# Queries of blocks 0 to 3 projected ahead of the third group's keys in a hybrid attention / mLSTM diffusion step

## The chip, the cores and the metric

The kernel runs on one core of one Trainium2 chip. The metric is device time in microseconds (us) of one execution; lower is better. The kernel before takes 1570.68 us, the median of three runs (1569.95 to 1571.53).

## The reference: what is computed

One layer of a hybrid backbone over 128 context tokens and 1024 latent tokens with 1024 features each. Cut to what matters here:

```
sh1, sc1, g1, sh2, sc2, g2 = split(silu(cond) @ w_ada + b_ada)       # adaLN, per kind of token
h  = rmsnorm(x, norm1_w) * (1 + sc1) + sh1
aq, ak, av, mq, mk, mv, mo, mg = split(h @ w_in)                      # widths 512,128,128,4 x 512,16
aq = rmsnorm(aq per head) ; ak = rmsnorm(ak per head)                 # 8 query, 2 key heads of 64
latent tokens: axial rotary on aq, ak; keys = own + cached
attn_o = softmax(aq ak^T / 8) av
hm  = bidirectional chunkwise mLSTM(mq, mk, mv, gates from mg)        # 4 heads of 128
x   = x + g1 * (concat(attn_o, rmsnorm(hm) * sigmoid(mo)) @ w_out)
x   = x + g2 * swiglu(rmsnorm(x) * (1 + sc2) + sh2)
```

The outputs are both token groups after a final norm, the context's keys and values, and the context's final mLSTM states.

## The kernel before

The 1152 tokens are nine blocks of 128 rows: block 0 is the context, blocks 1 to 8 are latent. Three blocks make a group (CB = 3, NCH = 3). Products of full precision are made from pairs: a float32 matrix is scaled by a power of two and split into a high float16 part and a low remainder, and each product is three matmuls (high times high, low weight times high, high weight times low).

A weight set of the input projection is an object of class `Scaled`. `ready()` loads its four raw pieces, takes sums of absolute values on ACT (L198), and finds the power of two through a small chain over DVE and PE (`power_scale`, tiles `isc` and `pv`, L164 to L176). `pairs()` makes high parts on ACT (L218, L221, L222) and low parts on DVE (L219, L137), each piece in a tile of the tag `ipair`, which has four slots. The raw pieces of all sets but the first are in the tag `iraw`, also four slots.

The stage that the change touches is the first 165 us:

- Loads on SP's queue: x of blocks 0 to 5, the key/value/gate weights (`kvg`, 272 columns), sixteen tiles of `w_ada`, x of blocks 6 to 8 (L279), then the query weights, and so on.
- Groups 0 and 1 are normalised and turned (transposed on PE, L116, copies at L371 and L372). The adaLN strips of shift and scale run on PE (L341), with a copy at L388.
- For each group c: `features(c)` forms the modulated, transposed tokens `hT` in pairs on ACT (L507) and DVE (L508, L137); then `linear_tok` projects the keys, values and gates of its three blocks (L483 to L485, 128x272). Behind the keys of group 0 stands `normalise(2)` (ACT squares L355, DVE scalings L358), behind those of group 1 `turn(2)`. Beside the keys of groups 1 and 2 run the steps of the query weights and of `ada`, a generator of the remaining adaLN loads (L423, 512 KB each, three buffers) and strips (L341).
- Then the pool of this stage is closed, a pool for the mLSTM is opened in its place, and the queries of all nine blocks are projected (L483 to L485, 128x512), in five groups `PAIRS` = (0, 1), (2, 3), (4,), (5, 6), (7, 8). Evacuating a group (`evac_q`) scales it (ACT, L724), normalises and rotates it over ACT, DVE and POOL (`norm_rope`, L664 to L686) and writes it to DRAM (`q_d`, L729, SP's queue).
- Beside the queries four generators are advanced, in the ratios 0.7, 1.15, 0.6, 0.3 of a step per unit of main work: `gates` (the gate chain from G to QT, L557 to L654), `ada`, `kwork` (key norms, key stacks `kst`, value parts), and the steps of the first mLSTM head's weights.
- Behind this the per-head projections (L808 to L810), the mLSTM scans and the attention follow, with PSUM pools that take the place of this stage's.

Python order gives each instruction a priority. A planner fixes each engine's order before the run from estimated times: of the instructions that it holds to be ready, the one of highest priority goes next; `hot(n)` moves the instructions inside it n places ahead. `weave(main, side, n_main, n_side)` interleaves two generators by count.

Of the kernel before, what the change touches and what calls it, by code (L numbers as in the profile page):

```python
# [19 lines left out]
P = 128  # L20
D = 1024
KD = D // P
NB = 9
# [22 lines left out]
def hybrid_step(ctx: ExitStack, tc: tile.TileContext, I: dict, O: dict):  # L46
# [11 lines left out]
    def nm(s):  # L58
        uid[0] += 1
        return f"{s}_{uid[0]}"  # L60
# [118 lines left out]
    class Scaled:  # L179
# [31 lines left out]
        def pairs(self, dve_every=2):  # L211
            out = []
            n, b = self.n, self.shape[1]
            for j, raw in enumerate(self.raws):
                w = wp.tile([P, 2, 1024], F16, name=nm("ipair"), tag="ipair", bufs=4)
# [162 lines left out]
    kvg_pairs = kvg.pairs(1)  # L378
# [119 lines left out]
    def features(c):  # L498
# [3 lines left out]
        for k in range(KD):  # L502
            full = p0.tile([P, CB, P], F32, name=nm("full"), tag="full", bufs=4)
            for i, n in ((0, 1), (1, 2)) if c == 0 else ((0, CB),):
                cnd = 0 if n == 1 else 1
                s, t = scale1[:, k, cnd : cnd + 1], shift1[:, k, cnd : cnd + 1]
                act(hh[:, k, i : i + n], v[:, k, i : i + n], AF.Identity, scale=s, bias=t)  # L507
                dve.tensor_scalar(out=full[:, i : i + n], in0=v[:, k, i : i + n], scalar1=s, scalar2=t, op0=ALU.mult, op1=ALU.add)  # L508
            sub(hl[:, k], full, hh[:, k], "dve")

    for c in range(NCH):
        with hot(100):
            features(c)
        prods = linear_tok(kvg_pairs, 0, 272, evac_kvg, (tuple(range(c * CB, c * CB + CB)),), bank if c == 1 else bankA)
        if c > 0:
            weave(prods, chain(steps, ada), KD, 10)
        else:
            emit(prods)
        if c == 0:
            normalise(2)  # L520
        if c == 1:
            turn(2)
    emit(steps)
    es0.close()
    mlp = es1.enter_context(tc.tile_pool(name="mlp", bufs=1, reuse_waits="tile"))
    mwh = mlp.tile([P, 512], F32, name="mwh")
    for tag, shape, bufs, dt in (("cs", [P, P + 1], CSB, F32), ("c0f", [P, P + 1], 2, F32), ("c0b", [P, P + 1], 1, F32), ("hm", [P, NB, P], 2, F32), ("ssh", [P, NB], 2, F32), ("nu", [P, 2, P + 1], 4, F32),
                                 ("it", [P, 2, P + 1], 3, F32), ("dn", [P, 2], 3, F32), ("jkh", [P, P], 1, BF16), ("sd", [P, 2, P], 4, F32),
                                 ("dt", [P, 2, P], 4, F32), ("so", [P, P], 9, F32), ("va", [P, P + 1], 9, F32), ("kT", [P, P], 9, F32),
# [1030 lines left out]
```

## Time and profile before

| | |
|---|---|
| median of three runs | 1570.68 us |
| profiled execution, own time | 1568.19 us |
| its span, first to last instruction | 1566.4 us |
| mean granted TensorE clock | 0.982 |
| PE busy | 1484.4 us (95%) |
| DVE busy | 1017.7 us (65%) |
| ACT busy | 771.7 us (49%) |
| POOL busy | 267.8 us (17%) |
| DMA moved | 236.91 MB, mean 151 GB/s |

Engines are PE (TensorE matmul), PEld (its weight loads, which overlap PE), DVE (VectorE), ACT (ScalarE), POOL (GpSimd) and SP (SyncE, which issues most DMAs); SPq is SP's queue. L483 is line 483 of the kernel before. In a row `out<-in` names the tiles, `x8` the count, and what stands in brackets is how long the engine stood idle before and what ended that. Ends of matmuls are modelled, so a busy PE is not PE at its peak; distances between starts tell the rate.

### The profile page before, as it was taken

The numbers are of one execution on the slowest core, as the hardware profiler recorded it, in microseconds if no ns is written. First come the engines' busy times: TensorE is split into PE (matmuls) and PEld (weight loads), VectorE is DVE, ScalarE is ACT, GpSimd is POOL, SyncE is SP. The second block draws the span as 40 slices with busy tenths as digits, with TensorE's granted clock in tenths as the row PEclk, the third lists the DMA queues.
The fourth block names the chain that finished last, engine by engine and source line by source line (L and its number), as shares of the span: only waits on it lengthen the run. The fifth ranks groups of instructions, "written<-read, shape, count | busy, mean of one in ns | idle before, by whom it ended". The sixth has DMA issues, their size and how long they took to land.

```text
span 1566.4 us, 23369 instructions
## 1 busy us (share of the span) xinstructions
PE 1484.4 (95%) x8539; PEld 1244.8 (79%) x8539; DVE 1017.7 (65%) x2007; ACT 771.7 (49%) x1413; POOL 267.8 (17%) x354
## 2 busy tenths in 40 slices
PE   6899999999999689999999999999999999999997
PEld 3544567677766468898998989989898989999996
DVE  4878554837669576677555677878866585554554
ACT  4754465847656344545432444556552443323333
POOL 0213333322343242100110101000010101001110
PEclk9899999999999799999999999999999999999999
DMA  9564323523657748767554547878773545534441
GB/s 362 177 190 156 100 68 41 130 38 68 122 148 170 254 80 201 182 182 170 153 154 144 152 126 237 195 172 178 176 169 114 168 129 175 162 117 139 148 139 63
DMA packets 387881, 236.91 MB, mean 151 GB/s; under 512 B 170198, under 2 KB 346790, under 8 KB 387766
## 3 DMA queue, kind: packets, MB, share of 16 engines
q1 hardware_dynamic: 385110, 231.84, 54.2%
q10 hardware_dynamic: 2656, 3.58, 1.1%
q8 instruction: 67, 1.10, 0.3%
q14 instruction: 48, 0.39, 0.1%
HBM read 183.79 MB, written 13.26 MB: 126 GB/s over the span
## 4 chain that ended last, share of the span: by engine, by line
PE 80%; DVE 9%; ACT 4%; DMA 4%; issue 2%; POOL 1%; SPq 0%; ACTq 0%; DVEq 0%; POOLq 0%
PE mm L1316 12%; PE mm L1317 11%; PE mm L1315 11%; PE mm L1115 5%; PE mm L1116 5%; PE mm L1117 5%; PE S L1035 4%; PE wi L485 3%; PE wi L484 3%; PE wi L483 3%; PE mm L1147 2%; PE mm L1148 1%; PE mm L1149 1%; PE mm L116 1%; PE po L1060 1%
## 5 line engine op out<-in xcount | busy, mean ns | idle before, releaser
L152 ACT CAST whi<-raw 128x1024 fp32r<-128x1024 f32 (+1 forms) x216 | 221.9, 1027 | 415.1 <-PE mm L1316 148.8
L137 DVE TENSOR_TENSOR wlo<-raw,whi 128x1024 fp32r<-128x1024 f32 (+1 forms) x216 | 259.9, 1203 | 204.9 <-ACT whi L152 204.4
L1316 PE MATMUL mm<-aTl,whi 128*128 128x384 f32 x1056 | 355.7, 337 | 2.7 <-DVE aTl L137 2.7
L1317 PE MATMUL mm<-aTh,wlo 128*128 128x384 f32 x1056 | 354.3, 336 | 0.0
L1315 PE MATMUL mm<-aTh,whi 128*128 128x384 f32 x1056 | 353.3, 336 | 0.0
L137 POOL TENSOR_TENSOR hl<-tn,hl 128x384 fp32r<-128x384 f32 x66 | 84.1, 1275 | 840.0 <-ACT hl L1338 757.3
L1316 PEld LDWEIGHTS mm<-aTl,whi 128*128 128x128 f32 x1056 | 198.5, 188 | 3.9 <-DVE aTl L137 3.3
L1315 PEld LDWEIGHTS mm<-aTh,whi 128*128 128x128 f32 x1056 | 198.1, 188 | 0.6
L1317 PEld LDWEIGHTS mm<-aTh,wlo 128*128 128x128 f32 x1056 | 198.4, 188 | 0.0
L1116 PE MATMUL mm<-wlo,hl 128*128 128x512 f32 x372 | 145.7, 392 | 0.0
L1115 PE MATMUL mm<-whi,hl 128*128 128x512 f32 x372 | 144.3, 392 | 0.0
L1117 PE MATMUL mm<-whi,hl 128*128 128x512 f32 x372 | 143.4, 392 | 0.0
L483 PE MATMUL wi<-ipair,hT 128*128 128x384 f16 (+2 forms) x408 | 135.2, 334 | 2.0 <-ACT hT L507 1.2
L484 PE MATMUL wi<-ipair,hT 128*128 128x384 f16 (+2 forms) x408 | 135.2, 334 | 0.0
L485 PE MATMUL wi<-ipair,hT 128*128 128x384 f16 (+2 forms) x408 | 132.0, 335 | 1.0 <-DVE hT L137 1.0
L1042 DVE SCALAR_TENSOR_TENSOR pl<-pr,st,ph 128x1152 f16<-128x1152 f32 (+1 forms) x72 | 94.8, 1317 | 33.9 <-ACT ph L1041 32.5
L1041 ACT ACTIVATE ph<-pr,st 128x1152 f16<-128x1152 f32 (+1 forms) x72 | 83.8, 1164 | 27.2 <-issue 7.2
L1037 DVE TENSOR_REDUCE st<-S 128x1 f32<-128x1152 f32 (+1 forms) x72 | 88.8, 1233 | 12.5 <-PE S L1035 12.3
L1038 ACT ACTIVATE pr<-S,st 128x1152 f32<-128x1152 f32 (+1 forms) x72 | 81.3, 1129 | 31.7 <-DVE st L1037 28.0
L1035 PE MATMUL S<-kst,qT 128*128 128x384 f32 (+1 forms) x400 | 86.8, 347 | 5.0 <-ACT pr L1038 5.0
L1104 DVE TENSOR_TENSOR t<-mm,gl 128x512 f32<-128x512 f32 x102 | 68.9, 685 | 26.2 <-DMA gl<-g_d 12.5
L1117 PEld LDWEIGHTS mm<-whi,hl 128*128 128x128 f32 x372 | 69.9, 188 | 14.2
(381 smaller groups left out, 2525.0 us busy)
## 6 DMA issues: line engine op xcount, KB each, us to landing
raw<-in_w_gu_dram SPq DMA_DIRECT2D x132, 512.0 KB
raw<-in_w_down_dram SPq DMA_DIRECT2D x60, 512.0 KB
a<-in_w_ada_dram SPq DMA_DIRECT2D x24, 512.0 KB
gl<-g_d SPq DMA_DIRECT2D x36, 256.0 KB
aw<-in_w_ada_dram SPq DMA_DIRECT2D x16, 512.0 KB
iraw<-in_w_in_dram SPq DMA_DIRECT2D x32, 256.0 KB
raw<-in_w_out_dram SPq DMA_DIRECT2D x12, 512.0 KB
x<-in_x_sample_dram SPq DMA_DIRECT2D x11, 512.0 KB
```

Source lines behind the costliest of these rows:

```text
L137: (dve if eng == "dve" else pool).tensor_tensor(out=out, in0=full, in1=hi, op=ALU.subtract)
L152: nc.scalar.copy(hi[:, :n], raw[:, :n])
L483: mm(ps[:, :n], ah, wh[:, k % 2, c0 : c0 + n], start=(k == 0), stop=False)
L484: mm(ps[:, :n], ah, wl[:, k % 2, c0 : c0 + n], start=False, stop=False)
L485: mm(ps[:, :n], al, wh[:, k % 2, c0 : c0 + n], start=False, stop=(k == KD - 1))
L1035: mm(S[:, n, 0:w], qT[:, h, :], kst[kv][:, t, c0 + n * w : c0 + (n + 1) * w], start=(t == 0), stop=(t == 1))
L1115: mm(ps, ah, wh[:, k % 2, :], start=(k == 0), stop=False)
L1116: mm(ps, ah, wl[:, k % 2, :], start=False, stop=False)
L1117: mm(ps, al, wh[:, k % 2, :], start=False, stop=(k == nk - 1))
L1315: mm(ps, wh[:, k, :], th[:, k, :], start=(k == 0), stop=False)
L1316: mm(ps, wh[:, k, :], tl[:, k, :], start=False, stop=False)
L1317: mm(ps, wl[:, k, :], th[:, k, :], start=False, stop=(k == KD - 1))
```

## The change

Four parts, all in the first stage:

1. The object of the query weights is made, and its loads are issued, ahead of the loads of x for blocks 6 to 8. Its sums and its scale are emitted ahead of the features.
2. The pairs of the key weights get tiles of their own (`kpair0` to `kpair3`) in the stage's pool `p0`, instead of the four `ipair` slots.
3. The order around the keys is written out. `normalise(2)` follows the keys of group 0, its ACT instructions behind the last one of `features(0)`; then the query weights' pairs are made and the first head's weights are loaded; the keys of group 1 are woven with four steps of `ada`, which has had one step before; `turn(2)`, `features(2)`; then the queries of blocks 0 to 3 and, behind these, the keys of group 2, woven with 27 steps of `ada`.
4. The remaining five blocks' queries (24 units instead of 40) run beside the four generators, with ratios 1.17, 1.15, 1.0 and 0.5.

`features` also returns its last ACT instruction. The loop over groups goes away; the opening of the mLSTM pool and the load of `mwh` stand behind the keys of group 2 as before. The diff's core:

```diff
-        def pairs(self, dve_every=2):
+        def pairs(self, dve_every=2, home=None):
...
-                w = wp.tile([P, 2, 1024], F16, name=nm("ipair"), tag="ipair", bufs=4)
+                w = home(j) if home else wp.tile([P, 2, 1024], F16, name=nm("ipair"), tag="ipair", bufs=4)
...
+    q_group = Scaled([[(full_view, rows_of(j)[:, :, 0:512])] for j in range(4)], (2, 512))
+    q_steps = q_group.ready()
+    next(q_steps)
     for b in range(2 * CB, NB):
         load_x(b)
...
-    kvg_pairs = kvg.pairs(1)
+    kvg_pairs = kvg.pairs(1, lambda j: p0.tile([P, 2, 544], F16, name=f"kpair{j}"))
...
-    groups_in = [Scaled([[(full_view, rows_of(j)[:, :, 0:512])] for j in range(4)], (2, 512))] + [head_group(h) for h in range(NH)]
-    steps = groups_in[0].ready()
-    next(steps)
+    groups_in = [q_group] + [head_group(h) for h in range(NH)]
+    emit(q_steps)
...
-    for c in range(NCH):
-        with hot(100):
-            features(c)
-        prods = linear_tok(kvg_pairs, 0, 272, evac_kvg, (tuple(range(c * CB, c * CB + CB)),), bank if c == 1 else bankA)
-        if c > 0:
-            weave(prods, chain(steps, ada), KD, 10)
-        else:
-            emit(prods)
-        if c == 0:
-            normalise(2)
-        if c == 1:
-            turn(2)
-    emit(steps)
...
+    next(ada)
     qp = es_r.enter_context(tc.tile_pool(name="qp", bufs=1, side="right", reuse_waits="tile"))
...
+    def keys(c):
+        return linear_tok(kvg_pairs, 0, 272, evac_kvg, (tuple(range(c * CB, c * CB + CB)),), bank if c == 1 else bankA)
+
+    with hot(100):
+        last = features(0)
+    emit(keys(0))
+    with tc.issue_after(last):
+        normalise(2)
+    with hot(100):
+        features(1)
+    w_q = q_group.pairs()
+    q_group.inverses()
+    steps = groups_in[1].ready()
+    next(steps)
+    weave(keys(1), ada, KD, 4)
+    turn(2)
+    with hot(100):
+        features(2)
+    evac = evac_q(qp, qcc, qss, qw)
+    weave(chain(linear_tok(w_q, 0, 512, evac, PAIRS[:2]), keys(2)), ada, 3 * KD, 27)
...
-    w_q = groups_in[0].pairs()
-    groups_in[0].inverses()
-    steps = groups_in[1].ready()
-    next(steps)
-    weave(linear_tok(w_q, 0, 512, evac_q(qp, qcc, qss, qw)), beside((gates, 0.7), (ada, 1.15), (kwork, 0.6), (steps, 0.3)), 40, 40)
+    weave(linear_tok(w_q, 0, 512, evac, PAIRS[2:]), beside((gates, 1.17), (ada, 1.15), (kwork, 1.0), (steps, 0.5)), 24, 24)
```

More of the change, by code (lines that the diff above doesn't have):

```diff
@@ L506, in features @@
                 s, t = scale1[:, k, cnd : cnd + 1], shift1[:, k, cnd : cnd + 1]
[L507 removed]
+                last = act(hh[:, k, i : i + n], v[:, k, i : i + n], AF.Identity, scale=s, bias=t)
                 dve.tensor_scalar(out=full[:, i : i + n], in0=v[:, k, i : i + n], scalar1=s, scalar2=t, op0=ALU.mult, op1=ALU.add)
             sub(hl[:, k], full, hh[:, k], "dve")
[L511 to L531 removed]
+        return last.ins
     def gate_work(mlp):
@@ L731, in evac_q @@
         return evac
-    dma(mwh, I["mlstm_norm_w"][0:1, :].to_broadcast([P, 512]))
-    dve.tensor_scalar(out=mwh, in0=mwh, scalar1=0.5, scalar2=None, op0=ALU.mult)
     def qcol(i, d, b, h):
```

12 lines of the change are left out of this document (10 added, 2 removed).

## The prediction

> **What bounds the kernel now.** I read the page's head first, then busy time by stretches of the span, cut where the order of the work changes: features and keys of the first two groups (46 to 67.7 us), turn, features and keys of the third (67.7 to 93, "the front"), the query projection (93 to 165.2, "the tail"), then everything behind it.
>
> ```profile
> span 1566.4 us, 23369 instructions
> PE 1484.4 (95%) x8539; PEld 1244.8 (79%) x8539; DVE 1017.7 (65%) x2007; ACT 771.7 (49%) x1413; POOL 267.8 (17%) x354
> ...
> 46.00:67.70 21.70, 20.42 (x144) 14.86 (x144) 21.70 (x58) 18.16 (x45) 6.61 (x6) 0.83 0.44 117
> 67.70:93.00 25.30, 20.67 (x174) 12.93 (x174) 22.38 (x75) 16.01 (x27) 4.83 (x5) 0.93 0.63 197
> 93.00:165.20 72.20, 66.28 (x407) 30.68 (x406) 55.20 (x189) 38.02 (x76) 16.63 (x11) 0.98 0.54 162
> 165.20:480.00 314.80, 305.80 (x1998) 219.21 (x1998) 187.19 (x499) 198.06 (x559) 108.88 (x222) 0.99 0.39 89
> ```
>
> The columns are the stretch, its length, busy time (and instructions) of PE, PEld, DVE, ACT and POOL, the granted clock, DMA share and GB/s. PE carries the kernel at 95%. From 46 to 67.7 us DVE is busy for all 21.70 us and sets the pace. From 67.7 on PE sets it, but with holes: 25.30 - 20.67 = 4.6 us in the front and 72.20 - 66.28 = 5.9 us in the tail. From 165.2 to 480 PE is busy 97% of the time, so I take a start there that is earlier by so many us as an end earlier by as many. The waits and the clock name the holes:
>
> ```profile
> PE mm L175 <- DVE pv L164: 2.3, 2, 1.4
> PE mm L341 <- DMA a<-in_w_ada_dram: 2.2, 3, 1.1
> PE mm L116 <- DVE isc L200: 1.0, 1, 1.0
> PE wi L483 <- ACT vall L493: 0.7, 1, 0.7
> ...
> PE mm L116 <- DVE ry L133: 3.7, 1, 3.7
> PE wi L808 <- DVE QT L654: 1.6, 1, 1.6
> ...
> 68.00:70.80 2.80, 0.66 (x3) 0.47 (x3) 2.70 (x21) 1.71 (x6) 0.00 (x0) 0.95 0.00 0
> 70.80:72.70 1.90, 1.90 (x17) 0.62 (x17) 1.76 (x14) 1.56 (x2) 0.22 (x1) 0.50 0.00 0
> 72.70:75.00 2.30, 2.30 (x22) 1.54 (x19) 0.69 (x3) 1.22 (x2) 0.65 (x2) 0.73 0.77 238
> 136.00:138.60 2.60, 2.59 (x9) 1.44 (x10) 2.37 (x10) 2.54 (x4) 1.83 (x1) 0.50 1.04 347
> ```
>
> A wait row gives the total, the times, and the longest. After a hole the granted clock is 0.50 to 0.73: the front loses 1.90 x 0.50 + 2.30 x 0.27 = 1.6 us by that, the tail 2.60 x 0.50 = 1.3. So the front wastes 4.6 + 1.6 = 6.2 us and the tail 5.9 + 1.3 = 7.2; these 13.4 us are all there is to win behind 67.7 us.
>
> **The change, part by part.**
>
> *Loads.* The four query weight loads go ahead of the last three rows of x.
>
> ```profile
> 27.67 3.23 SPq L279 DMA_DIRECT2D x<-in_x_sample_dram  x3
> 34.29 4.21 SPq L193 DMA_DIRECT2D iraw<-in_w_in_dram  x4
> ...
> 40.00:46.00 6.00, 2.80 (x19) 2.44 (x19) 3.16 (x24) 4.53 (x11) 0.00 (x0) 0.77 1.05 393
> ...
> 39.60 0.58 ACT L388 COPY part<-wi 128x512 f32<-128x512 f32 x1 [9.86 <-PE wi L341]
> 45.50 11.91 ACT L507 ACTIVATE hT<-x,shift,scale 128x128 f16<-128x128 f32 x24 [0.37 <-DVE shift L402]
> ```
>
> SP issues the rows at 27.67 and the weights at 34.29, and the DMA engines are full (1.05) up to 46 us at 393 GB/s. The weights are 2.1 MB, 5.3 us at that rate; the rows come that much later, the weights 3 x 0.52 MB, 4 us, earlier. The rows' squares no longer run at 40 us but behind the first group's features, as the change orders them itself, so their lateness costs nothing. This is the one wait that is added: on ACT the squares stand behind the features that run from 45.50 to 57.4, and behind the squares stand the key evacuations and the pairs; DVE's row scalings wait for them, but DVE is full with features up to 66.6 anyway. The eight absolute-value sums move to where the squares were, with 9.86 us of ACT idle ahead of 39.60. If such a sum stands before the copy there or the first features at 45.50 in ACT's order and its weights are late, the start slips: from 0 to 1.3 us, the time of one such load at 393 GB/s. I take 0.3, as the loads come 4 us earlier. Behind it, the query weights' scale is known by about 50 us, and the waits on isc and pv at 67.7 to 70.4 (1.0 + 1.4) lose their cause.
>
> *Key weights' pairs in own tiles.* No instruction is added; the query weights' pairs no longer wait for slots which the third group's keys still read. They move from about 90 us to just behind DVE's full stretch, whose end is
>
> ```profile
> 66.57 2.07 DVE L358 TENSOR_SCALAR x<-x,ry 128x1024 f32<-128x1024 f32 x3
> ```
>
> The first piece's low part can only come behind the features and these three row scalings, near 69.5 us; PE has only adaLN strips until then. Bounds of that hole: 0.5 us (strips fill it) to 4.6 (as wide as the front's holes now). I take 2.0.
>
> *Queries of blocks 0 to 3 into the front.* The adaLN strips by forms, in the tail and in the front; the query products in the front, one of their three lines; and the starts of two of them:
>
> ```profile
> L341 PE MATMUL mm<-a,silp 128*32 128x256 f32 x128 | 10.4, 390 | 0.0
> ...
> L341 PE MATMUL mm<-a,silp 128*32 128x256 f32 x64 | 6.4, 455 | 2.2 <-DMA a<-in_w_ada_dram 2.2
> L485 PE MATMUL wi<-ipair,hT 128*128 128x512 f16 x2 | 0.8, 379 | 0.0
> ...
> 109.78 0.38 PE L483 MATMUL wi<-ipair,hT 128*128 128x512 f16 x1
> 110.00 0.38 PE L484 MATMUL wi<-ipair,hT 128*128 128x512 f16 x1
> ```
>
> Starts are 0.216 us apart, so four blocks of 24 matmuls are 4 x 24 x 0.216 = 20.7 us; some 8 of these (2 to 3 on each line, 1.7 us) ran in the front already: 19.0 us move. The third group's keys end after 1 + 4 + 27 = 32 adaLN steps of 55, some 14 of 24 loads' strips; now 64 of 192 strip matmuls, 8 loads, lie ahead of 93 us. Six loads' strips, at 10.4 / 16 = 0.65 us each, move too, and some columns, 0.5: 4.4 us. PE's work at full clock becomes 20.7 - 1.6 + 19.0 + 4.4 = 42.5 us in the front and 66.3 - 1.3 - 23.4 = 41.6 in the tail. Instructions, PSUM evacuations and DMAs stay the same in number. POOL's part of the two groups moves along, into a front where POOL is busy 4.83 of 25.30 us, at no cost.
>
> DVE decides whether PE can keep that pace:
>
> ```profile
> L679 DVE TENSOR_TENSOR nr<-qraw,ss 128x256 f32<-128x256 f32 x8 | 4.0, 553 | 2.0 <-POOL qraw L668 2.0
> L666 DVE TENSOR_REDUCE nrs<-nr 128x16 f32<-128x1024 f32 x3 | 3.6, 1217 | 1.8 <-ACT nr L664 1.8
> L131 DVE TENSOR_TENSOR rt<-ry 128x16 f32<-128x16 f32 x9 | 2.7, 304 | 0.1
> L686 DVE TENSOR_TENSOR qraw<-qraw,nr 128x1024 f32<-128x1024 f32 x1 | 1.2, 1206 | 0.0
> ```
>
> Normalising two groups of query blocks is 2 x 1.22, 24 small ones at 0.17 to 0.30 (say 0.27, 6.5), six L679 at 0.55 (3.3) and 1.9 of L686 (1.2 and half of it): 14.1 us. With one weight pair's low part (1.2, a 128x1024 operation like L686's) and adaLN's small ones some 16 us move, so the front has 22.4 + 16 = 38.4 us of DVE to 42.5 of PE (90%), the tail 39.2 to 41.6 (94%); the tail now has 55.2 to 65.0 (85%) and wastes 7.2 / 65.0 = 11%. Front: the 2.0 us hole, 0.5 where the keys' third bank waits for a query evacuation (0.7 now for its like), and a clock loss. Tail: 11% x 94/85 x 41.6 = 5.1; bounds 0.5 (no hole but the last) to 15.5 (below).
>
> *The clock.* The row at 70.8 shows 0.50 although PE, in the 2.8 us before, was busy 0.66 us and waited no more than 1.4 us at a time. So a 2 us hole can still bring slow time, and I leave half of the front's 1.6 us, 0.8. The Trainium skill, "TensorE: Matmul & The Clock Gate", section "What's actually happening", has the clock halved only after an idle window of about 3.4 us; this row does not bear that out, as the wait was shorter and broken. By that page the 0.8 would fall away and the sum come 0.8 lower; the row decides.
>
> *SP's queue.* The order of loads on it changes: four query weights earlier, the first head's eight loads at about 70 instead of 89 us, four query blocks' writes among the adaLN loads.
>
> ```profile
> SPq L423 <- PE mm L341: 41.3, 15, 12.5
> SPq L729 <- DVE qraw L686: 21.2, 4, 12.3
> ```
>
> A write waits up to 12.3 us for its normalising, and adaLN loads queue behind it. Their rate is that of the tail now (27 steps to 24 units against 1.15 to one), where PE waited for none. I take 0, bounds 0 to 5 us. The gates' and the keys' steps are only packed into 24 units instead of 40.
>
> **Sum.** Front 6.2 - (2.0 + 0.5 + 0.8) = 2.9 us won, tail 7.2 - 5.1 = 2.1 won, start 0.3 lost: 4.7 us. The profiled execution took 1568.19 us (span 1566.4), 2.5 below the median of 1570.68; the difference is put on the median: 1566.0.
>
> **Rivals.**
>
> *The gates' chain sets the end (slower).* It starts with the last keys' gate columns and ends with QT, whose copy releases PE at the stage's end (the 1.6 us wait above). The steps of PE, and the results that they use:
>
> ```profile
> 96.65 0.36 DVE L496 SCALAR_TENSOR_TENSOR G<-wi,isc,gbias 128x8 f32<-128x8 f32 x2 [0.15 <-ACT vall L493]
> 113.22 0.15 DVE L581 COPY ends<-cm 64x1 f32<-64x1 f32 x1
> ...
> 122.01 0.38 PE L116 MATMUL mm<-ident,ends 128*1 128x128 f32 x2
> ...
> 135.31 0.31 ACT L620 ACTIVATE dec<-dec 1x128 f32<-1x128 f32 x1 [7.17 <-DVE dec L619]
> ...
> 148.67 0.48 PE L624 MATMUL mm<-dec,one 1*128 1x128 f32 x2
> ...
> 151.00 0.31 ACT L639 ACTIVATE qe__1707<-qe__1707 128x128 f32<-128x128 f32 x1
> ...
> 162.53 0.31 PE L116 MATMUL mm<-ident,ai 128*128 128x128 f32 x1
> ```
>
> From 97.0 to 165.2 it takes 68 us, under 65 us of PE work. Three pauses ahead of PE's steps are 113.4 to 122.0, 135.6 to 148.7 and 151.3 to 162.5: 33 us; bare it is 35 us. Afterwards only 41.6 us of PE work cover it, while DVE's 39.2 us stand in the same queue. Should two thirds of the pauses stay, it takes 35 + 22 = 57, the tail wastes 15.5, and the kernel is 15.5 - 7.2 - 2.9 + 0.3 = 5.7 us slower: 1576. It turns to a loss when the chain is over 41.6 + 7.2 + 2.6 = 51 us. For it: DVE at 94%. Against: the pauses are PE's order, and the rates of the gates' steps are raised.
>
> *No change.* SP blocks behind a query write and PE waits some 5 us for adaLN weights in the front: 1571. For: three such waits (2.2 us) now; against: none in the tail, at the same rate.
>
> *All holes close.* DVE's moved work fits everywhere: 13.4 less 2: 1559. Against: DVE at 90% and more throughout.
>
> **How the numbers follow.** 0.2% (3.1 us) is about what a measurement tells from no change. My forecast, 1566 (1561 to 1567.5), has 0.40, all holes closed 0.15, no change 0.17, the gates' chain 0.28. Faster is then 0.55, same 0.17, slower 0.28. The range from 1558.5 to 1577 takes in the first rival's price and the full closing, and leaves out a longer chain and a gain past 12 us, 2 in 10.
>
> **What would show it.** Right: PE without waits on isc and pv near 68 us; 128x512 query matmuls from about 70 us; the third keys' end near 113; first head matmuls near 160.5 us instead of 165.2. The tail step fails if PE waits for QT or key transposes for over 10 us together; the load step if the features start after 45.8; the SP step if adaLN waits exceed 2.2 us. A shift behind 165 us of another size than at 165 would make the prediction wrong as well.

## The result, and the profile after

The changed kernel is slower: 1579.03 us (median of six runs, 1577.01 to 1580.36) against 1570.32 us for the kernel before beside it (1569.48 to 1574.25). The ratio is 1.0057, 95% interval 1.0044 to 1.0069. The forecast was 1566.0 with a range up to 1577. The profiled execution took 1578.23 us, its span is 10.0 us longer than before's. First the page's head:

```profile
span 1576.4 us, 23369 instructions
...
PE 1486.6 (94%) x8539; PEld 1245.2 (79%) x8539; DVE 1013.8 (64%) x2007; ACT 771.5 (49%) x1413; POOL 269.5 (17%) x354
```

The instructions are the same in number and the engines as busy as before; the 10 us are waiting and slow clock. To place them, I cut both spans alike into three stretches: the start (46 to 68 us), the front (68 to 132) and the tail (132 to 180). The columns are those of the prediction's table. Before:

```profile
46.00:68.00 22.00, 20.44 (x144) 14.86 (x144) 22.00 (x59) 18.46 (x46) 6.61 (x6) 0.83 0.43 116
68.00:132.00 64.00, 58.98 (x413) 29.45 (x413) 48.92 (x183) 33.29 (x63) 12.08 (x11) 0.97 0.60 184
132.00:180.00 48.00, 42.31 (x261) 22.86 (x254) 39.81 (x107) 26.43 (x49) 13.65 (x8) 0.96 0.46 139
```

After:

```profile
46.00:68.00 22.00, 15.70 (x91) 10.94 (x92) 21.64 (x70) 19.83 (x41) 8.44 (x6) 0.73 0.43 112
68.00:132.00 64.00, 64.00 (x462) 32.66 (x461) 37.83 (x114) 30.48 (x62) 10.82 (x9) 0.98 0.63 192
132.00:180.00 48.00, 37.44 (x213) 19.94 (x210) 42.76 (x153) 25.76 (x49) 12.36 (x9) 0.86 0.40 116
```

What TensorE wastes in a stretch is its length less PE's busy time multiplied by the granted clock: before 22.00 - 20.44 x 0.83 = 5.0, 6.8 and 7.4 us; after 10.5, 1.3 and 15.8. So the front wins 5.5 us, as it was meant to, the start loses 5.5 and the tail 8.4: together 8.4 of the 10.0 us are lost by 180 us. Behind that TensorE's order of instructions, from head 0's first score product on, is the old one but for three places.

The forecast had its own stages: the front up to the end of the third keys, and the tail from there to the first head product. In the changed kernel these are the stretches up to 119.4 and up to 172.4 us; the third column of busy time is DVE's:

```profile
67.70:119.40 51.70, 51.70 (x370) 27.16 (x368) 28.80 (x69) 23.94 (x49) 8.96 (x6) 0.98 0.58 178
119.40:172.40 53.00, 42.44 (x268) 21.37 (x268) 46.30 (x178) 30.66 (x61) 12.08 (x10) 0.90 0.53 159
```

The start's loss is one wait. First PE's longest between 47 and 70 us, then, in the order of time, DVE's steps of the scale's chain:

```profile
PE mm L175 <- DVE pv L164: 5.4, 1, 5.4
```

```profile
54.66 0.15 DVE L200 TENSOR_REDUCE isc<-isc 128x1 f32<-128x8 f32 x1
...
59.02 0.27 DVE L171 TENSOR_REDUCE pv<-mm 1x1 f32<-1x128 f32 x1
...
61.21 0.14 DVE L161 TENSOR_SCALAR pv<-pv 1x1 f32<-1x1 f32 x1
...
62.85 0.13 DVE L162 TENSOR_SCALAR pv<-pv 1x1 int32<-1x1 int32 x1
...
63.78 0.13 DVE L164 TENSOR_SCALAR pv<-pv 1x1 f32<-1x1 f32 x1
```

The scale's product (L175) stands in PE's order ahead of the second group's keys. It waits for a chain of six small DVE steps, 0.13 to 0.27 us each, and one transposition on PE (57.04 us, between the first two of them). DVE does its steps one at a time between the features of group 1: from 54.66 to 63.91 us, 9 us for under 1 us of DVE work. Behind the wait the keys run at half the rate:

```profile
58.19 0.28 PE L486 MATMUL wi<-kpair,hT 128*128 128x272 f16 x1
58.31 0.28 PE L487 MATMUL wi<-kpair,hT 128*128 128x272 f16 x1
63.97 0.58 PE L175 MATMUL mm<-pv,one 1*128 1x2 f32 x2 [5.38 <-DVE pv L164]
...
65.36 0.43 PE L486 MATMUL mm<-kpair,hT 128*128 128x272 f16 x1
65.58 0.43 PE L487 MATMUL mm<-kpair,hT 128*128 128x272 f16 x1
```

PE's longest waits in the tail, from 132 to 180 us, and behind them the ACT squares with which each of the eight norms begins:

```profile
PE mm L344 <- DMA a<-in_w_ada_dram: 6.2, 1, 6.2
PE mm L350 <- ACT part L444: 1.5, 1, 1.5
PE mm L116 <- ACT qe__1787 L618: 1.4, 1, 1.4
PE mm L116 <- DVE kall L665: 1.1, 1, 1.1
```

```profile
94.63 1.06 ACT L643 ACTIVATE nr<-qraw 128x1024 f32<-128x1024 f32 x1
108.36 1.06 ACT L643 ACTIVATE nr<-qraw 128x1024 f32<-128x1024 f32 x1
121.56 0.31 ACT L643 ACTIVATE nr<-kall 128x128 f32<-128x128 f32 x1 [1.10 <-DVE qraw L665]
123.69 0.63 ACT L643 ACTIVATE nr<-kall 128x512 f32<-128x512 f32 x1 [1.82 <-DVE nrs L645]
138.50 0.63 ACT L643 ACTIVATE nr<-kall 128x512 f32<-128x512 f32 x1 [7.10 <-DVE kall L665]
155.15 0.63 ACT L643 ACTIVATE nr<-qraw 128x512 f32<-128x512 f32 x1 [0.68 <-DVE kall L665]
169.94 1.06 ACT L643 ACTIVATE nr<-qraw 128x1024 f32<-128x1024 f32 x1
183.46 1.06 ACT L643 ACTIVATE nr<-qraw 128x1024 f32<-128x1024 f32 x1 [7.35 <-DVE qraw L665]
```

Every norm, of keys (`kall`) or of queries (`qraw`), squares into one scratch tile, `nr`: tag `nr0`, one buffer, handed out in program order. In the kernel before the key norms were emitted ahead of the query norms, and their squares ran at 60, 69 and 98 us; the last square of the eight came at 175.1:

```profile
59.99 0.32 ACT L664 ACTIVATE nr<-kall 128x128 f32<-128x128 f32 x1
69.04 0.66 ACT L664 ACTIVATE nr<-kall 128x512 f32<-128x512 f32 x1
98.03 0.65 ACT L664 ACTIVATE nr<-kall 128x512 f32<-128x512 f32 x1
...
175.08 1.06 ACT L664 ACTIVATE nr<-qraw 128x1024 f32<-128x1024 f32 x1 [2.21 <-DVE qraw L686]
```

Now two query norms precede them in program order. The scratch stands unused until 94.63 us, and then the line has no gap of more than 1.3 us (each square follows the last use of the scratch by the norm before it). DVE is busy 37.83 us of the front in place of 48.92, and must do the rest later; the first head product comes at 172.37 us in place of 165.19.

### The profile page after: what moved, and what is told of

Same layout as the page of the kernel before. It is cut to its first block, busy times and chain, and to the rows that moved or that the text cites. A ratio compares the mean times of both kernels' runs of the same rounds, so it can differ in the third digit from the quotient of the medians.

```text
span 1576.4 us, 23369 instructions
## 1 busy us (share of the span) xinstructions
PE 1486.6 (94%) x8539; PEld 1245.2 (79%) x8539; DVE 1013.8 (64%) x2007; ACT 771.5 (49%) x1413; POOL 269.5 (17%) x354
## 4 chain that ended last, share of the span: by engine, by line
PE 80%; DVE 9%; DMA 4%; ACT 4%; issue 2%; SPq 0%; POOL 0%; DVEq 0%; ACTq 0%; POOLq 0%
PE mm L1319 11%; PE mm L1320 11%; PE mm L1318 11%; PE mm L1118 5%; PE mm L1119 5%; PE mm L1120 5%; PE S L1038 4%; PE wi L485 3%; PE wi L487 3%; PE wi L486 3%; PE mm L1150 2%; PE mm L1151 2%; PE mm L1152 1%; PE po L1063 1%; PE po L1062 1%
## 5 line engine op out<-in xcount | busy, mean ns | idle before, releaser
L485 PE MATMUL wi<-ipair,hT 128*128 128x384 f16 (+1 forms) x360 | 121.3, 337 | 0.4 <-DVE qT L790 0.2
L486 PE MATMUL wi<-ipair,hT 128*128 128x384 f16 (+1 forms) x360 | 121.2, 337 | 0.0
L487 PE MATMUL wi<-ipair,hT 128*128 128x384 f16 (+1 forms) x360 | 121.2, 337 | 0.0
```

Of the source, the lines that this page charges most:

```text
L485: mm(ps[:, :n], ah, wh[:, k % 2, c0 : c0 + n], start=(k == 0), stop=False)
L486: mm(ps[:, :n], ah, wl[:, k % 2, c0 : c0 + n], start=False, stop=False)
L487: mm(ps[:, :n], al, wh[:, k % 2, c0 : c0 + n], start=False, stop=(k == KD - 1))
```

## The experiments

My theories were: the scale's wait makes the start's loss (scale theory); the key norms behind the query norms make the tail's (line theory). Rivals: the order of SP's queue, by which the last adaLN load stands behind six raw loads of the next head (the 6.2 us wait); later the gates' chain, VectorE's total of work, and the order behind the heads. The table has what TensorE wastes in each stretch, in us, worked out as above.

Each row's waste comes from one execution. The eleven runs in which the scale's steps have a higher priority have the same TensorE order up to 66 us, and still their start's waste lies between 5.4 and 7.4 us. So a difference of some 2 us between two rows is not told from chance.

| run | ratio to before (95%) | start | front | tail |
|---|---|---|---|---|
| before | 1 | 5.0 | 6.8 | 7.4 |
| changed kernel | 1.0057 (1.0044 to 1.0069) | 10.5 | 1.3 | 15.8 |
| hot_scale | 1.0052 (1.0035 to 1.0069) | 5.4 | 0.2 | 17.3 |
| own_scratch | 1.0052 (1.0036 to 1.0068) | 11.1 | 1.3 | 10.9 |
| early_keys | 1.0042 (1.0022 to 1.0063) | 11.2 | 1.9 | 11.9 |
| late_keys (on before) | 1.0122 (1.0096 to 1.0147) | 5.4 | 6.7 | 25.9 |
| ada_sooner | 1.0138 (1.0110 to 1.0167) | 10.7 | 1.3 | 14.3 |
| own_hot_ada | 1.0038 (1.0024 to 1.0053) | 5.5 | 0.0 | 21.2 |
| keys_first | 1.0066 (1.0049 to 1.0083) | 10.6 | 7.8 | 6.0 |
| keys_first_hot | 1.0037 (1.0024 to 1.0050) | 7.4 | 6.5 | 4.5 |
| one_pair_hot | 1.0019 (1.0007 to 1.0031) | 6.0 | 0.4 | 15.0 |
| warm_gates | 1.0064 (1.0043 to 1.0085) | 5.5 | 0.2 | 18.0 |
| one_early_hot | 1.0040 (1.0026 to 1.0053) | 6.4 | 3.7 | 15.6 |
| one_own_hot | 1.0037 (1.0025 to 1.0048) | 6.8 | 1.1 | 15.4 |
| newton_after | 1.0051 (1.0033 to 1.0069) | 11.0 | 0.6 | 12.1 |
| newton_before (on before) | 1.0017 (1.0000 to 1.0033) | 4.9 | 8.6 | 5.7 |
| one_more_ada | 1.0007 (0.9993 to 1.0021) | 5.6 | 1.6 | 16.9 |
| one_less_ada | 1.0021 (1.0007 to 1.0035) | 7.2 | 0.2 | 16.4 |
| late_first_S | 1.0014 (1.0003 to 1.0024) | 6.8 | 1.6 | 13.3 |
| late_S_early | 1.0026 (1.0014 to 1.0039) | 5.7 | 5.1 | 11.9 |

**The scale's steps ahead of the features**

```diff
-    emit(q_steps)
+    with hot(400):
+        emit(q_steps)
```

> The changed kernel, with the steps that find the query weights' scale given a higher priority than the features of groups 0 and 1 (priority 400), so that the eight abs-sums on ACT and the five small DVE steps go between features of group 0. The scale theory (TensorE's product for the scale stands ahead of group 1's keys and waits 5.4 us for a chain of small DVE steps that go one by one between group 1's features) expects the wait gone or under 1 us, keys of group 1 begun before 61 us at a clock over 0.9, and 4 to 6 us back: 1573 to 1575, while the tail stays as it is (the 6.2 us wait for the adaLN load). The rival that the features of group 1 themselves are late, and that the product only stood ahead of a wait that would have come anyway, expects a wait of 3 to 5 us for hT in its place and 1577 to 1579.

The start's waste fell from 10.5 to 5.4 us, the kernel before's value; PE's three largest waits from 46 to 180 us:

```profile
PE mm L116 <- DVE kall L666: 3.6, 1, 3.6
PE S L1039 <- DVE qT L137: 3.0, 1, 3.0
PE mm L175 <- DVE pv L164: 1.5, 1, 1.5
```

The scale theory holds for its place, with 1.5 us of the wait left where under 1 was expected. For the time it failed: 1576.98 us, ratio 1.0052, instead of 1573 to 1575. The first head product came at 162.61 us, 2.6 ahead of the kernel before, and by 180 us that lead was gone in waits for key norms and for qT (the turned queries, which head 0's first score product needs).

**Key norms out of the line, ahead of it, and behind it**

own_scratch gives the key norms `QT` and `decb`, not in use yet, as scratch:

```diff
...
+    class Fixed:
+        at = {}
+
+        def tile(self, shape, dt, name=None, tag=None, bufs=1):
+            if tag == "nr0":
+                return QT.rearrange("p t x -> p (t x)")
+            o = 16 * self.at.setdefault(tag, len(self.at))
+            v = decb[:, o : o + 16]
+            return v.bitcast(dt) if dt != F32 else v
+
-    kwork = chain(k_work(qp, kcc, kss, kw), key_stacks(), value_parts())
+    kwork = chain(k_work(qp, kcc, kss, kw, Fixed()), key_stacks(), value_parts())
```

> The changed kernel, with the key norms' scratch (the tile of tag nr0 and the small columns rv, ry, rt, rh, nrs) laid into the tiles QT and decb, which are free then, in place of the tiles that the query norms use too. Order of emission and arithmetic stay. The scratch theory (the key norms run at 123 to 138 us because they queue for one scratch tile behind the query norms of blocks 0 to 3) expects the key norms back before 95 us, DVE busy over 35 of the 51.7 us from 67.7 on (28.8 in the changed kernel) and under 41 of the 53 after them (46.3), the first head matmul some 6 us sooner than 172.4, and a time 5 to 8 us under the changed kernel's 1579.0: 1571 to 1574. The theory that the tail is held by the order of SP's queue (the last adaLN load behind six raw loads) expects the 6.2 us wait for that load to stay and a time of 1577 to 1579. The 5.4 us wait on the scale product stays in both.

early_keys leaves the one scratch and emits the first two key norms sooner:

```diff
     weave(keys(1), ada, KD, 4)
+    kwork = chain(k_work(qp, kcc, kss, kw), key_stacks(), value_parts())
+    next(kwork)
+    next(kwork)
     turn(2)
...
-    kwork = chain(k_work(qp, kcc, kss, kw), key_stacks(), value_parts())
```

> The changed kernel with the first two key norms (block 0 with the cache row, blocks 1 to 4) emitted between the second keys and the turn of the third group, so that they go through the scratch tile while it is free, and the query norms behind them. The wait on the scale stays. The line theory expects the two norms done before 95 us, the last square of the line some 12 to 17 us sooner than 183.5 (166 to 172), TensorE's loss between 145 and 180 us under 10 us in place of 14.3, and a time of 1570 to 1575, unless the planner's order behind the heads changes for the worse. Without it 1577 to 1580.

late_keys is the kernel before, with the key norms emitted later, and with them the key stacks and value parts that stand behind them in the same chain:

```diff
-    kwork = chain(k_work(qp, kcc, kss, kw), key_stacks(), value_parts())
+    def late(gen, n):
+        for _ in range(n):
+            yield
+        yield from gen
+
+    kwork = chain(late(k_work(qp, kcc, kss, kw), 12), key_stacks(), value_parts())
```

> The kernel before, with one thing of the changed kernel alone: the key norms are emitted behind the norms of the queries of blocks 0 to 3 (12 empty steps ahead of the key work in the last weave). Nothing is loaded, swapped or re-homed. The line theory says that the eight norms (three of keys, five of queries) go one after the other through the one scratch tile of tag nr0, some 11 to 16 us each, and that the end of this line sets when the last query group leaves its buffers and the attention of head 0 can start: in the kernel before the line has two key norms behind it by 85 us and its last square at 175.1 us, in the changed kernel it begins at 94.6, has no gap, and its last square stands at 183.5. It expects the last square at 182 to 190 us here, TensorE 6 to 12 us more idle between 132 and 180 us than in the kernel before (7.1 us of it lost there), and 1576 to 1583. The rival, that the swap and the wait on the scale make the loss and the place of the key norms is harmless, expects 1569 to 1572.

The later place of the key norms, and of what follows them, costs the kernel before 1.22%, 19 us, more than the changed kernel loses in all (1586.67 us against the 1576 to 1583 expected). The longest wait, the tail and the last square, from the slowest of its four executions (1593.05 us):

```profile
PE mm L116 <- DVE kall L686: 17.0, 1, 17.0
```

```profile
132.00:180.00 48.00, 28.02 (x168) 14.99 (x167) 34.30 (x118) 24.45 (x48) 12.47 (x11) 0.79 0.39 117
```

```profile
191.12 1.06 ACT L664 ACTIVATE nr<-qraw 128x1024 f32<-128x1024 f32 x1 [8.90 <-DVE qraw L686]
```

The 17.0 us are a wait for the key norms themselves (`kall`); in the changed kernel PE waits for these only 1.1 us in the tail. So the run shows that the place can cost that much; it does not show by which wait the changed kernel pays for it.

In the other direction the tail's waste falls from 15.8 to 10.9 us with own scratch and to 11.9 with the earlier place; the last square comes at 176.77 and 178.84 us in place of 183.46. So by 180 us these repairs give back 4 to 5 of the 8.4 us that the tail loses; in the time they do not show (ratios 1.0052 and 1.0042 against 1.0057, with intervals that overlap). My numbers were too good: 166 to 172 us was expected for the last square of early_keys, and both times stayed at 1577.57 and 1576.55 us. Without the key norms in the line the query norms took longer: in own_scratch the second last began at 146.76 and ended at 176.7. With own scratch the 6.2 us wait for the adaLN load is gone as well, and another adaLN wait is in its place:

```profile
PE mm L350 <- ACT part L444: 4.7, 1, 4.7
```

But the planner also drew up SP's order anew. In the changed kernel the last adaLN load stood behind six raw loads:

```profile
154.54 5.06 SPq L193 DMA_DIRECT2D iraw<-in_w_in_dram  x6
159.70 0.45 SPq L426 DMA_DIRECT2D a<-in_w_ada_dram  x1
```

With own scratch it stands ahead of them:

```profile
151.12 0.40 SPq L426 DMA_DIRECT2D a<-in_w_ada_dram  x1
159.58 4.66 SPq L193 DMA_DIRECT2D iraw<-in_w_in_dram  x4
```

In early_keys it is ahead of them too, at 156.93 us. So these two runs do not part the line theory from the queue theory: what they give back may in part be the load's earlier place.

**adaLN strips sooner, and all three edits together**

```diff
-    weave(linear_tok(w_q, 0, 512, evac, PAIRS[2:]), beside((gates, 1.17), (ada, 1.15), (kwork, 1.0), (steps, 0.5)), 24, 24)
+    weave(linear_tok(w_q, 0, 512, evac, PAIRS[2:]), beside((gates, 1.17), (ada, 1.7), (kwork, 1.0), (steps, 0.5)), 24, 24)
```

> The changed kernel, with the ratio at which adaLN strips are woven into the query tail raised from 1.15 to 1.7: the last adaLN loads then stand ahead of the next head's raw loads in SP's queue. The queue theory expects the 6.2 us wait for the load gone, the first head matmul at 165 to 166 us, and 6 to 8 us back: 1571 to 1573. The scratch theory expects the wait to move onto the gates' chain, the key stacks or the next head's weights, which were ready only at 168 to 172 us: 0 to 3 us back, 1576 to 1579.

> All three edits together: own scratch for the key norms, priority for the scale steps, ratio 1.7 for the adaLN strips. If scale wait and scratch order explain the loss, 10 to 13 us come back: 1566 to 1569, under the kernel before (1570.3). If a part of the loss has another cause (the weave itself, or loads moved), the time stays at 1571 or over.

ada_sooner has no wait for the load, but 4.3 us for the gates' chain (qw) and 2.5 for an adaLN shift; the tail's waste is 14.3 instead of 15.8. So the load's place is worth 1.5 us here, within the spread of the rows, and not the 6 to 8 of the queue theory: the load was the last of several that came late. The 1591.07 us are a second matter. Behind the heads this ratio gave TensorE another order (over 100 places of difference to the kernel before), and waste grew there too (from 540 to 580 us 18.1 us, before 9.1); neither theory had that. All three edits together gave 1574.65, not 1566 to 1569: the start is good (5.5), the front perfect (0.0), and the tail the worst but one (21.2). The repairs do not add. This run also speaks against the line as the tail's bound: its last square is at 160.42 us, 23 us sooner than in the changed kernel, and TensorE stood all the same, 5.1 us of it until the gates' QT was copied and 3.1 for an adaLN shift.

**The swap undone, the rest kept**

```diff
-    weave(chain(linear_tok(w_q, 0, 512, evac, PAIRS[:2]), keys(2)), ada, 3 * KD, 27)
+    weave(keys(2), ada, KD, 10)
...
-    weave(linear_tok(w_q, 0, 512, evac, PAIRS[2:]), beside((gates, 1.17), (ada, 1.15), (kwork, 1.0), (steps, 0.5)), 24, 24)
+    weave(linear_tok(w_q, 0, 512, evac), beside((gates, 0.7), (ada, 1.15), (kwork, 0.6), (steps, 0.3)), 40, 40)
```

> The changed kernel with the swap alone undone: the third group's keys are projected ahead of all queries again, and the last weave has the kernel before's five query groups and ratios; the early load of the query weights, their scale ahead of group 1's keys and the own tiles of the key weights' pairs stay. The chain theory (the gates' chain starts from G, which needs the third keys; the swap moved G's transposes from 99.8 to 125.6 us; from them to the tile QT the chain took 46.7 us in the changed kernel, and of 45.2 to 47.9 in the four runs before this one, so the heads cannot start before G plus some 45 us, and the queries that would fill TensorE meanwhile have been used up) expects G's transposes at 98 to 106 us, QT not after 167, the first head matmul at 165 to 168, and 1570 to 1574: back to the kernel before but for the 5.4 us wait on the scale. A theory in which the loss comes from the loads, the tiles or the scale wait, and not from the swap, expects 1576 to 1580.

> The run above with the scale's steps at higher priority. The chain theory and the scale theory together expect G's transposes before 100 us, the first head matmul before 165.2 us (the kernel before), and 1564 to 1569. If the early scale is worth nothing without the swap, 1570 to 1572.

```profile
46.00:68.00 22.00, 15.61 (x89) 10.77 (x90) 21.99 (x85) 19.89 (x42) 9.09 (x6) 0.73 0.47 115
68.00:132.00 64.00, 59.21 (x413) 33.21 (x411) 43.62 (x133) 28.55 (x59) 11.81 (x10) 0.95 0.55 165
132.00:180.00 48.00, 43.74 (x274) 22.16 (x273) 39.33 (x121) 27.07 (x51) 11.56 (x7) 0.96 0.51 152
```

This pair prices the swap. Against the changed kernel keys_first (rows above) has the same start, a front that wastes 6.5 us more and a tail that wastes 9.8 less: the swap costs 3.3 us net by 180 us. With the scale's steps at higher priority the sums are 18.4 us (keys_first_hot) and 22.9 (hot_scale): 4.5. By the times the swap is not shown to cost anything: the ratios without it are 1.0066 and 1.0037, with it 1.0057 and 1.0052. G's transposes came at 109.8 and 104.3 us, and QT only at 173.8 and 167.2, so the 45 us of the chain theory do not hold where the chain is not hurried. The times were 1581.78 and 1576.98, not 1570 to 1574 and 1564 to 1569: both runs lose again behind 180 us. keys_first_hot is level with the kernel before there, and its waits between 180 and 220 us are new, where TensorE's order behind the heads is another one (some 50 places). The longest:

```profile
PE S L1039 <- ACT pr L1042: 3.2, 1, 3.2
```

So a time cannot be read here without the waste by stretches: a change in the front also makes the planner draw up the later order anew.

**One query pair ahead; the gates' chain ahead**

one_pair_hot is hot_scale with `PAIRS[:1]` in place of `PAIRS[:2]` (18 adaLN steps over 2 * KD), and 32 units with ratios 0.88, 1.15, 0.75, 0.38 in the last weave. warm_gates is hot_scale with each step of the gates' chain under `hot(200)`.

> The changed kernel with the scale's steps at higher priority, and with the queries of blocks 0 and 1 alone ahead of the third keys; those of blocks 2 and 3 stand in the last weave again, which has 32 units in place of 24. The chain theory expects G's transposes some 8 us sooner than in the run with two pairs and the same priority (116.7), at 107 to 110 us, QT at 153 to 158, TensorE idle under 3 us between G and the first head matmul, that matmul at 158 to 161 us, and 1565 to 1570. A theory in which VectorE's total work sets the start of the heads, wherever G stands, expects QT at 161 to 164 and 1572 to 1575, as in the run with two pairs.

> The changed kernel with the scale's steps at higher priority, and the gates' chain at priority 200 too, so that its small VectorE steps go ahead of the query and key norms. If the 45 us from G to QT are queueing on VectorE, they shrink to 35 to 40 and the heads' first matmul moves ahead of 160 us, while the key stacks and norms that were pushed back wait for it: 1571 to 1575. If they are the chain's own length and the pace of the weave, QT stays at 160 to 163 and the time at 1575 to 1577.

With one pair G's transposes came at 105.62 us (116.73 with two), QT at 154.5 (161.9), the first head product at 156.58: the chain moved as the chain theory said, even sooner than expected. The time did not follow, 1573.07: TensorE then stood at the first score product of head 0 (6.4 us for qT). warm_gates left QT at 162.7 and took 1580.93: the 45 us from G to QT are not queueing that a priority removes. The gates' chain is one of the things that are late, not the last one.

**One pair, with the key norms repaired**

one_early_hot and one_own_hot are one_pair_hot with the edit of early_keys and of own_scratch.

> Scale steps at higher priority, queries of blocks 0 and 1 alone ahead of the third keys, and the first two key norms early as above. The line theory expects the line to end some 10 us sooner than in the run with one pair (last square 176.4): 163 to 170, the 6.4 us wait for qT gone or under 2 us, TensorE's loss from 145 to 180 us 6 to 9 us in place of 14.9, and 1564 to 1569, under the kernel before. If VectorE's work or the gates' chain is the bound, 1571 to 1574 as with one pair.

> As the run before, but with the key norms taken out of the line by own scratch (QT and decb) in place of an earlier place in the order. The line theory expects nearly the same: last square 163 to 171, 1564 to 1570. If it is the order of emission that matters and not the tile, the last square stays at 174 to 178 and the time at 1571 to 1574.

1573.6 and 1575.53, a miss for both: the last squares at 174.77 and 173.74 (163 to 171 expected), the tails 15.6 and 15.4 as with one pair alone (15.0). The 6.4 us for qT are gone, and waits for adaLN's sums are there (L350 3.0 and 5.6 us).

**The norms' small steps cut**

```diff
-    def rsqrt(tp, ss, n, inv, cap=16, plus=EPS):
+    def rsqrt(tp, ss, n, inv, cap=16, plus=EPS, steps=3):
...
-        for _ in range(3):
+        for _ in range(steps):
...
-        r = rsqrt(qp, ssum, n, 1.0 / HD)
+        r = rsqrt(qp, ssum, n, 1.0 / HD, steps=1)
```

> The changed kernel, with two of the three refinements of the reciprocal square root left out in the key and query norms (six small VectorE steps of about 0.2 us in each of the eight norms, so the norms are less exact). The VectorE theory (46 to 172 us hold a fixed amount of VectorE work, and the changed kernel does 8.2 us less of it by 172 us than the kernel before, because the key norms, and what hangs on them, have to wait for the query norms; TensorE's loss by 180 us is 8.5 us larger) expects 6 to 8 us of VectorE work and latency cut to come back nearly whole in the tail: TensorE's loss between 145 and 180 us 6 to 9 us in place of 14.3, the last square of the line at 172 to 177, and 1570 to 1574. If the gates' chain or SP's queue holds the tail, 1577 to 1580.

> The same cut in the kernel before. TensorE has only 2.0 us to lose between 145 and 180 us there and 5.0 between 132 and 145, so the VectorE theory expects less than half of what the cut gives in the changed kernel: 1566 to 1570 against 1569 to 1571 of the kernel before. If the norms' small steps bound both kernels alike, both gain the same.

The last square moved from 183.46 to 176.15 and the tail's waste from 15.8 to 12.1 us: half of what the VectorE theory expected. The kernel before's tail gained 1.7 and its front lost 1.8. In newton_after, too, the last adaLN load stands ahead of the raw loads, at 148.95 us. Neither time moved down (1579.3, 1573.77); both have other orders behind the heads, and whether these took the gain is not shown. So cutting the norms gives back less than their work.

**The order behind the heads kept, and one product moved**

one_more_ada is one_pair_hot with 22 adaLN steps in the front in place of 18; one_less_ada has (ada, 1.0) in place of (ada, 1.15). With both TensorE's order from head 0's first score product on is the kernel before's but for three places. late_first_S adds to one_more_ada:

```diff
             for h in range(NQ):
-                with hot(ha):
+                with hot(ha if b or h else 0):
```

> One query pair ahead of the third keys and the scale at higher priority, as in one_pair_hot (1573.1), with 22 adaLN steps in place of 18 woven into the front; the planner then leaves TensorE's order behind the first head product as in the kernel before. The theory of the new order behind the heads expects the 2.6 us that one_pair_hot loses behind 180 us (2.5 behind the kernel before at 180 us, 5.1 at 700) to come back: 1569 to 1571. If those losses come with the later start of the heads and not with the order, 1572 to 1574.

> As the run before, but with the ratio of the adaLN steps in the tail at 1.0 in place of 1.15 (and 18 in the front), which also leaves the order behind the heads as in the kernel before; the remaining adaLN steps come together at the end of the tail. Theory of the new order: 1569 to 1572; of the later start: 1572 to 1574.

> As one_more_ada (one query pair ahead of the third keys, scale's steps at higher priority, 22 adaLN steps in the front), with the first score product of block 0 emitted without its priority, so that it stands 39 places later among the head products in TensorE's order; the order behind is left but for four places. The order theory (the lead is given back because TensorE's fixed order puts that product ahead of head products that are ready) expects the 9.4 us wait for qT at 3 us or less, TensorE's loss up to 180 us some 3 to 6 us under that of the kernel before (1.8 over it in one_more_ada), and 1564 to 1568: faster than the kernel before (1570.5 in the last session) and than the changed kernel. The shortage theory (the heads' own inputs are late as well: weight pairs, adaLN sums) expects the wait to move to ipair or wi and 1571 to 1574.

With the order kept, one_more_ada is not to be told from the kernel before (1.0007, 0.9993 to 1.0021); by its 1573.56 us the later-start theory had it, by the ratio it is undecided. one_less_ada, with 1574.12 us and 1.0021, lies next to the later-start theory's 1572 to 1574. The largest wait of one_more_ada from 46 to 180 us, then that of late_first_S, and the ACT copy of the query tile (`qraw`) that releases it:

```profile
PE S L1039 <- DVE qT L137: 9.4, 1, 9.4
```

```profile
PE wi L785 <- ACT qraw L704: 4.4, 1, 4.4
```

```profile
166.10 1.25 ACT L704 ACTIVATE qraw<-wi,isc 128x512 f32<-128x512 f32 x2
```

Moving that one product back took the 9.4 us away, and TensorE went on to a head product whose PSUM bank still held the last query group. Its copy out (L704) runs at 166.10 us, right behind the square at 165.15 of the group before it in the line. The tail's waste fell from 16.9 to 13.3; the time, 1571.34 (ratio 1.0014), is no gain on the kernel before. The shortage theory had both the wait and the time.

late_S_early adds the edit of early_keys, with 18 steps and a ratio of 1.0 for adaLN:

> As late_first_S, with the first two key norms emitted between the second keys and the turn of the third group, and the adaLN steps at 18 in the front and a ratio of 1.0 in the tail, by which TensorE's order behind the heads stays near that of the kernel before (14 places of difference). The line theory expects the last query group's copies out of its banks before 162 us (166.1 in late_first_S), the wait for qraw gone, TensorE's loss up to 180 us 3 to 6 us under that of the kernel before, and 1563 to 1567. If the adaLN sums or the gates' chain end as late as the norms, one of them takes the wait over and the time is 1569 to 1572.

```profile
PE mm L350 <- ACT part L444: 4.4, 1, 4.4
PE mm L116 <- DVE scale L336: 3.1, 1, 3.1
```

No wait for qraw is left, and adaLN's sums have taken its place, the rival of the expectation; the copies came at 163.9, not before 162. No version beat the kernel before.

## Why the prediction was wrong

Set side by side, the forecast had the start 0.3 us longer, the front 2.9 and the tail 2.1 shorter, and nothing behind 165 us. Measured, by the stretches above, are 5.5 longer, 5.5 shorter, 8.4 longer, and 1.6 longer behind 180 us. Two steps failed, the scale's wait and the tail.

*Loads, right at the front and wrong behind it.* The features started at 45.45 us (limit 45.8). But "the waits on isc and pv lose their cause" failed: I took the scale as known by 50 us because its loads came early, and did not ask where its six small DVE steps stand in DVE's order, nor that PE's product now stands ahead of the second keys. The waits near 68 us are gone, and one of 5.4 stands at 58: 4.7 us more idle and 0.8 more of slow clock in the start, of which hot_scale brings 5.1 back. The first query product came at 76.81 us instead of about 70 (in hot_scale at 69.50), and the third keys ended at 119.4 rather than 113 (in hot_scale at 111.2): both late by the scale's wait.

*Key weights' pairs, right.* I allowed a hole of 2.0 us near 69.5; PE has none in the front.

*Queries into the front, the front right, the tail wrong.* The front's waste fell by 5.5 us (forecast 2.9). The step that failed is the split of DVE's work, 38.4 us in the front and 39.2 in the tail; measured are 28.8 and 46.3. The query norms did move into the front, but some 6.6 of the 22.4 us that DVE had there were steps of the first two key norms, and these now run behind 119 us. "The gates' and the keys' steps are only packed into 24 units" hid it: their place in program order fell behind two query norms, and with one scratch tile a later place is a later time. With the split the tail's waste of 5.1 failed: it is 15.8 us, at the forecast's own upper bound of 15.5. late_keys shows that the place can cost that much; own_scratch and early_keys give 4 to 5 us back by 180 us, in which the earlier adaLN load has a part that is not parted off. The swap itself, by keys_first, won 6.5 and lost 9.8.

*SP, outside its bounds.* I took 0 (bounds 0 to 5) and the adaLN wait was 6.2. Without it (ada_sooner, own_scratch) other waits of 4 to 5 us stand there, so the load is not the whole of the tail's loss.

*The clock.* I left 0.8 us in the front; 1.3 were wasted there, with PE busy throughout: it is the end of the slow clock behind the 5.4 us wait. Half speed stood behind the two new waits, of 5.4 and 6.2 us. There the trace agrees with the rule of the Trainium skill ("TensorE: Matmul & The Clock Gate", "What's actually happening"), as both are longer than its idle window of some 3.4 us.

*The rivals.* "The gates' chain sets the end" named the sign and nearly the size (1576), and not the mechanism. From G to QT the chain took 51.3 us, shorter than before's 68; by that rival's own sum 51 us is where a loss begins, and its 1576 asks for 57. PE waited no 10 us for QT. That the size came near is luck. One of its two conditions, DVE's queue, was part of it. The test "a shift behind 165 us of another size" failed too: 7.2 us at the first head product, 10.0 at the end; 1.9 of the difference are slow clock between 172 and 180 us (8.00 us of work at 0.76).

*Open.* The start's loss is shown, by the wait and by hot_scale. Of the tail's 8.4 us, 4 to 5 come back with the key norms' place or tile, together with an earlier adaLN load; how much is which is not shown, nor does the time follow. For the rest, and for why every version with queries in the front gives its lead back between 145 and 180 us, the runs show a row of things that come within some 10 us of each other (QT, the last query group's copy, qT, adaLN's sums, the next head's pairs): where one was hurried, another held TensorE. Which would be the last is not settled. That VectorE's total sets it (8.5 us less done by 180 us, 8.4 wasted more) is argued, not shown; newton_after gave half of what that asks.

## What to carry to other kernels

Filling a hole on the busiest engine pays only if what the filled stage feeds comes no later: here 5.5 us were won in the front and 8.4 lost in the tail, where other chains end. Before moving a step in program order, list every single-buffered tile it shares with steps that it passes: the scratch tile of one buffer put all eight norms in one line, in program order, and in the changed kernel ACT stood 7 us idle before two of the squares. An edit meant for one engine can change another's order too (here SP's loads); look there before giving the gain to the edit. And ask where each small step of a dependent chain stands in the order of a full engine: six steps of 0.13 to 0.27 us, with one transposition among them, took 9 us.

## What the runs showed that I had not expected

- Half speed lasts long behind a wait. Behind the 5.4 us one the key products' starts were 0.22 us apart instead of 0.12 up to 69 us; behind the 6.2 us one TensorE had 8.44 us of work in 12 at a clock of 0.51:

```profile
164.00:176.00 12.00, 8.44 (x36) 5.25 (x37) 10.85 (x37) 9.12 (x21) 1.26 (x1) 0.51 0.37 109
```

- A change in the first 100 us can move later stages by several us, as the planner draws up their order anew: keys_first_hot was level with the kernel before at 180 us and ended 9.7 us of span behind it (6.6 by the medians), with another order there. That the order is the reason is argued, not shown.
